# A Strassen–Winograd MLP: unread sums not stored, other sums stored a superblock earlier, an x cast issued earlier, an accumulator in its own tile

## The chip, the cores and the metric

The kernel runs on one core of one Trainium2 chip. The metric is device time in microseconds (us). A smaller time is better.

Names used below: TensorE does the matrix products (PE in the profile), VectorE (DVE) the additions, ScalarE (ACT) copies and gelu, GpSimd (POOL) issues stores to memory, SyncE (SP) issues loads. A "gap" is time in which TensorE sits idle. The granted clock is the share of full speed that TensorE was allowed (1.00 is full). A load or store "lands" when the profile shows its completion.

## The reference

```python
# x: 8 x 1024 x 1024, w1: 1024 x 4096, w2: 4096 x 1024, all float32
def reference(x, w1, w2):
    h = x @ w1
    h = 0.5 * h * (1 + np.tanh(np.sqrt(2 / np.pi) * (h + 0.044715 * h ** 3)))
    return (h @ w2).astype(np.float32)
```

## The kernel before

The 8192 rows of x are taken in eight superblocks of 1024 rows, numbered 0 to 7. In each, two large products (x by w1, then gelu, then by w2) are done with Winograd's form of Strassen's scheme: seven half-size products instead of eight, with sums and differences of blocks as operands. The operand sums of the weights are the same in every superblock, so they are made once on VectorE, stored in device memory and loaded ready-made later.

- w1 is cut in four "quads" of four column chunks. Each quad has four raw blocks (products 2 and 5 use two of them as they are) and five sums, numbered 4, 1, 3, 7, 6.
- w2 has the same five sums. Sums 6 and 7 of w2 are products that are themselves split once more (`split_inner`, stored in `in_d`), so nobody reads the copies of these two sums in `w2_d`.

The first product, cut to what matters. A `MadeQuad` loads raw blocks and makes sums on VectorE; `load_ops` loads the ready operands.

```python
# first product, matmul1
def ahead(q, step):                 # prepares quad q, a part for each chunk of quad q-1
    if q == NI // QC:
        return
    if sb > 2:                      # ready sums from memory
        if step == 0:
            quads.append(load_ops(w1_d[q], raw_d[q], ORDER, KH, QW))
        return
    if step == 0:                   # raw blocks, sums made here; stored in superblock 2
        quad = MadeQuad(q, sb == 0, sb == 2)
        quads.append(quad)
        # ... (superblock 0: load from w1)
    for m in ((), (4,), (1, 3), (7, 6))[step]:
        quads[q].sum(m)             # VectorE, then a store on GpSimd's queue if asked for

for c in range(NI):                 # 16 chunks
    q, j = divmod(c, QC)
    if j == 0:
        ahead(q + 1, 0)
    # ... seven products of the chunk; VectorE combines their results:
    c11 = temp()
    tt(c11, u, rb, ADD)             # the chunk's last combination
    gelu("11", c, c11)
    late = (c, w, qb, s2)
    if j:
        ahead(q + 1, j)             # sums of the next quad
```

The second product of superblocks 0 and 1 (later superblocks use another routine, which loads ready sums):

```python
# matmul2_made
def add(m, over=None):              # one sum of w2, in four pieces
    u, op, v = B_TERMS[m]
    sums[m] = []
    for q in range(NI // QC):
        t = unit(QC, OH) if over is None else raw[over][q]
        tt(t, raw[u][q], raw[v][q], op)
        sums[m].append(t)
        if sb:
            nc.gpsimd.dma_start(out=w2_d[q][:, m - 1, :], in_=flat(t))

# ... products 4 first
u, d = {}, {}
for q, ps in product2(g, 2, pieces(2), pb, False):
    at, d[q] = copy_out("21", q, ps)         # d[q] is one of 10 shared temporaries
    if q == 1:
        xb = x_cast(sb + 1, at)              # casts the next superblock's x, in memory
add(1)
for q, ps in product2(g, 5, pieces(5), qb, True):
    tt(u[q], u[q], ps, SUB)
    tt(d[q], u[q], d[q], SUB)
add(7, over="21")
blocks = x_transpose(xb, load_in_order)
for q, ps in product2(g, 1, pieces(1), rb, True):
    tt(d[q], d[q], ps, ADD)                  # d accumulates output block 22
if sb:
    split_inner(7, pieces(7))
for q, ps in product2(g, 7, pieces(7), rb, False):
    tt(u[q], u[q], ps, ADD)
    store(sb, "11", q, u[q])
# ... products 3 and 6; the last one ends with
    tt(d[q], d[q], ps, ADD)
    last = store(sb, "22", q, d[q])
```

Two buffer pools matter. `tmp` has 10 temporaries of 128 x 512 float32. `u` has 26 buffers for weight operands, blocks of x and staging. A tile scheduler orders the instructions of each engine and inserts the waits for buffers.

## Time and profile before

| | before |
|---|---|
| median of 3 runs | 1582.91 us (1581.23 to 1582.93) |
| span of the profiled execution | 1577.2 us (that execution: 1579.01 us) |
| TensorE busy | 1547.1 us, 98% |
| superblock 0, 1, 2 | 204.53, 195.17, 197.34 us |
| superblocks 3 to 6 | 190.5 us each |

The lengths of superblocks are read from the timeline of TensorE, from the start of one first product to the start of the next. The 190.5 us of a superblock without a gap is the measure for the others.

The first part of the page of before. The columns are busy time, share of the span and number of instructions.

```profile
span 1577.2 us, 20360 instructions
PE 1547.1 (98%) x7808; PEld 767.1 (49%) x7808; DVE 1028.8 (65%) x1291; ACT 467.9 (30%) x784; POOL 202.8 (13%) x290
```

TensorE is the limit. Only the gaps can be won, about 30 us, and some 11 us of these are start-up. The timeline of TensorE for before follows: start, length, engine, line, operation, and in brackets the gap ahead of it and what ended the gap.

```profile
173.87 20.89 PE L567 MATMUL ps<-u,gc 128*128 128x512 f16 x96 [3.02 <-DVE gc L112]
...
222.22 97.37 PE L285 MATMUL ps<-u 128*128 128x512 f16 x448
...
333.79 41.60 PE L567 MATMUL ps<-u,gc 128*128 128x512 f16 x192 [0.38 <-DVE tmp L443]
375.94 13.99 PE L567 MATMUL ps<-u,gc 128*128 128x512 f16 x64 [0.56 <-DVE gc L112]
...
417.39 9.09 PE L285 MATMUL ps<-u 128*128 128x512 f16 x40
431.00 19.20 PE L285 MATMUL ps<-u 128*128 128x512 f16 x80 [4.52 <-ACT tmp L349]
```

The first product of superblock 1 (222.22) runs without a gap worth listing. In superblock 2 TensorE stops for 4.52 us ahead of 431.00. The releaser named is a ScalarE copy, but that is only the last link. VectorE's timeline for before shows the first:

```profile
419.81 2.06 DVE L112 TENSOR_TENSOR tmp<-tmp,ps 128x512 f32<-128x512 f32 x3
427.39 1.22 DVE L112 TENSOR_TENSOR u<-u 128x2048 f16<-128x2048 f16 x1 [5.53 <-DMA u<-raw_d]
428.54 1.28 DVE L112 TENSOR_TENSOR tmp<-tmp,ps 128x512 f32<-128x512 f32 x2
430.98 0.69 DVE L112 TENSOR_TENSOR tmp<-tmp,ps 128x512 f32<-128x512 f32 x1 [1.17 <-ACT tmp L349]
```

`u<-u` at 427.39 is a w1 sum for a later quad. VectorE stood 5.53 us in front of it for a raw block still on its way. The combinations `tmp<-tmp,ps`, which free TensorE's accumulators, stand behind it in the same queue. The table by stage of before (stretch, its length, busy time of each engine with instruction counts; the last three numbers are granted TensorE clock, DMA share and GB/s) shows what surrounded it:

```profile
426.00:430.00 4.00, 0.48 (x3) 0.10 (x1) 2.42 (x3) 0.15 (x1) 1.09 (x3) 1.00 1.02 416
430.00:432.00 2.00, 1.00 (x5) 0.46 (x5) 1.02 (x2) 0.95 (x2) 1.10 (x3) 0.95 1.25 406
432.00:434.00 2.00, 2.00 (x6) 0.69 (x5) 1.41 (x3) 1.24 (x3) 1.03 (x3) 0.50 1.02 330
434.00:436.00 2.00, 2.00 (x8) 0.83 (x7) 0.66 (x2) 0.47 (x1) 0.77 (x2) 0.70 1.04 242
```

DMA was saturated, and after the gap the clock was low. What is missing from full clock in the three stretches from 430 to 436 us (0.05, 0.50 and 0.30 of 2 us each) is 1.7 us, as much as 3.4 us at half clock. One more line of before: the same kind of sum in superblock 1, on VectorE, where the wait was short enough to do no harm.

```profile
227.40 1.23 DVE L112 TENSOR_TENSOR u<-u 128x2048 f16<-128x2048 f16 x1 [1.70 <-DMA u<-raw_d]
```

### The profile page before, as it was taken

To read this page: it belongs to the slowest core of one execution; us is meant where nothing else is said; L and a number is where in the kernel's file an instruction comes from. 1 tells how busy PE (TensorE), PEld (TensorE's weight loads), DVE (VectorE), ACT (ScalarE), POOL (GpSimd) and SP (SyncE) were. 2 spreads that over 40 slices of the span, in tenths; PEclk is the share of its full clock that TensorE was granted. 3 is DMA by queue.
4 is the path that set the end of the run, shared out by engine and by line. 5 is a ranking of instruction groups with operands and counts; after the bars stand their busy time and mean duration, and the time that the engine had idled before them with its cause. 6 is when DMAs were issued, how large, how long until landed. Compare 5 with 4: busy or idle time off the path is not lost.

```text
span 1577.2 us, 20360 instructions
## 1 busy us (share of the span) xinstructions
PE 1547.1 (98%) x7808; PEld 767.1 (49%) x7808; DVE 1028.8 (65%) x1291; ACT 467.9 (30%) x784; POOL 202.8 (13%) x290
## 2 busy tenths in 40 slices
PE   7999999999899999999999999999999999999998
PEld 4444444444344455444554445544554445544454
DVE  6875967678775567555665647656575556655564
ACT  4645024410144111441124410344004430044210
POOL 2241010033310012000120001200121001200000
PEclk9999999999999999999999999999999999999999
DMA  9999852399965567735696446954569445663164
GB/s 303 340 327 340 246 205 97 122 302 327 399 184 144 200 252 271 233 107 191 247 314 200 157 153 246 358 151 179 179 239 355 135 186 192 243 234 134 54 233 167
DMA packets 165634, 352.64 MB, mean 224 GB/s; under 512 B 72736, under 2 KB 78880, under 8 KB 164640
## 3 DMA queue, kind: packets, MB, share of 16 engines
q1 hardware_dynamic: 146944, 278.97, 51.1%
q0 software_dynamic: 18592, 72.37, 13.9%
q8 instruction: 61, 1.00, 0.3%
q14 instruction: 37, 0.30, 0.1%
HBM read 272.63 MB, written 93.32 MB: 232 GB/s over the span
## 4 chain that ended last, share of the span: by engine, by line
PE 86%; DMA 8%; DVE 3%; issue 1%; ACT 1%; POOL 0%; SPq 0%; DVEq 0%; ACTq 0%; POOLq 0%
PE ps L285 47%; PE ps L567 33%; PE ps L523 6%; DMA u<-w_d 2%; DVE u L112 2%; DMA u<-raw_d 2%; DMA gc<-in_w_dram 1%; DVE tmp L112 1%; DMA out_dram<-tmp 1%; DMA in_d<-u 1%; DVE gc L112 1%; DMA w_d<-u 1%; DMA xb<-in_x_dram 0%; DMA u<-in_x_dram 0%; DMA u<-in_d 0%
## 5 line engine op out<-in xcount | busy, mean ns | idle before, releaser
L285 PE MATMUL ps<-u 128*128 128x512 f16 x3584 | 782.1, 380 | 10.5 <-ACT tmp L349 4.5
L112 DVE TENSOR_TENSOR tmp<-tmp,ps 128x512 f32<-128x512 f32 x580 | 395.8, 685 | 301.4 <-ACT tmp L349 113.7
L285 PEld LDWEIGHTS <-u 128*128 128x128 f16 x3584 | 351.5, 98 | 438.6 <-issue 17.2
L567 PE MATMUL ps<-u,gc 128*128 128x512 f16 x1792 | 389.7, 379 | 3.9 <-DVE gc L112 3.6
L567 PEld LDWEIGHTS <-gc 128*128 128x128 f16 x1792 | 175.2, 98 | 216.0 <-DVE gc L112 4.6
L295 ACT ACTIVATE g<-tmp 128x512 f16<-128x512 f32 x256 | 161.0, 630 | 287.4 <-DVE tmp L112 287.4
L567 PE MATMUL ps<-u,g 128*128 128x512 f16 x1024 | 223.6, 379 | 0.0
L112 DVE TENSOR_TENSOR u<-u 128x2048 f16<-128x2048 f16 (+2 forms) x170 | 183.4, 1112 | 20.9 <-DMA u<-raw_d 12.3
L295 ACT ACTIVATE g<-ps 128x512 f16<-128x512 f32 x256 | 151.8, 596 | 98.4 <-PE ps L285 97.8
L567 PEld LDWEIGHTS <-g 128*128 128x128 f16 x1024 | 100.2, 98 | 119.6
L112 DVE TENSOR_TENSOR gc<-g,g 128x2048 f16<-128x2048 f16 x112 | 132.9, 1220 | 15.8 <-PE ps L567 15.8
L112 DVE TENSOR_TENSOR u<-u,ps 128x512 f32<-128x512 f32 x144 | 95.7, 681 | 68.7 <-ACT tmp L624 37.3
L381 POOL DMA_DIRECT2D out_dram<-tmp x72 | 39.5, 548 | 778.4 <-ACT tmp L617 593.1
L523 PE MATMUL ps<-u,gc 128*128 128x256 f16 x960 | 109.8, 273 | 0.7
L349 ACT COPY tmp<-ps 128x512 f32<-128x512 f32 x128 | 73.0, 570 | 95.5 <-PE ps L285 95.5
L523 PEld LDWEIGHTS <-gc 128*128 128x128 f16 x960 | 93.8, 98 | 12.8 <-issue 1.8
L112 DVE TENSOR_TENSOR gc<-u 128x2048 f16<-128x2048 f16 x60 | 73.2, 1219 | 39.3 <-PE ps L567 39.3
L112 DVE TENSOR_TENSOR tmp<-ps,tmp 128x512 f32<-128x512 f32 x128 | 88.2, 689 | 5.9 <-PE ps L285 1.1
L112 DVE TENSOR_TENSOR u<-tmp,ps 128x512 f32<-128x512 f32 x24 | 16.5, 687 | 74.8 <-PE ps L567 65.1
L112 DVE TENSOR_TENSOR u<-g,g 128x2048 f16<-128x2048 f16 x48 | 59.4, 1277 | 0.0
L617 ACT COPY tmp<-ps 128x512 f32<-128x512 f32 x24 | 14.1, 586 | 152.0 <-PE ps L567 152.0
L624 ACT COPY tmp<-ps 128x512 f32<-128x512 f32 x24 | 14.0, 585 | 133.5 <-PE ps L567 132.8
(32 smaller groups left out, 351.0 us busy)
## 6 DMA issues: line engine op xcount, KB each, us to landing
u<-w_d SPq DMA_DIRECT2D x172, 512.0 KB, 7.8
u<-raw_d SPq DMA_DIRECT2D x136, 512.0 KB, 7.1
u<-in_d SPq DMA_DIRECT2D x84, 512.0 KB, 6.8
gc<-in_w_dram SPq DMA_DIRECT2D x48, 512.0 KB, 6.5
w_d<-u POOLq DMA_DIRECT2D x40, 512.0 KB, 7.3
out_dram<-tmp POOLq DMA_DIRECT2D x72, 256.0 KB, 3.8
raw_d<-u SPq DMA_DIRECT2D x32, 512.0 KB, 10.0
xb<-in_x_dram POOLq DMA_DIRECT2D x56, 256.0 KB, 11.0
```

The source lines that it names most:

```text
L112: nc.vector.tensor_tensor(out=out, in0=in0, in1=in1, op=op)
L285: nc.tensor.matmul(bank, lhsT=ops[m][:, k, cs], rhs=xs[m][:, k, :], start=(first and k == 0), stop=(k == KH - 1), skip_group_check=not first,)
L295: gelu_last[0] = nc.scalar.activation(out=g[b][:, c, :], in_=src, func=GELU)
L349: nc.scalar.copy(out=v, in_=pb)
L381: return queue.dma_start(out=out2[r0:r0 + P, o0:o0 + OH], in_=src)
L523: nc.tensor.matmul(bank[:, i * HO:(i + 1) * HO], lhsT=t[:, c, i * P:(i + 1) * P], rhs=y[j][:, c, :], start=(first and i == 0 and c == 0), ...
L567: nc.tensor.matmul(banks[q], lhsT=a, rhs=pieces[c // QC][:, c % QC, :], start=(first and c == 0), stop=(c == NI - 1), skip_group_check=not ...
L617: nc.scalar.copy(out=c21, in_=ps)
L624: nc.scalar.copy(out=c12, in_=ps)
```

## The change

Its intent is to unload superblocks 1 and 2. It has four parts:

1. Sums 6 and 7 of w2 are no longer stored (nobody reads them): eight stores of 512 KB fewer.
2. The sums of w1 quads 1 to 3 are stored in superblock 1, so superblock 2 loads them ready. Only quad 0 stays as it was: 15 VectorE sums fewer.
3. The x cast for superblock 2 stands in the program at the start of superblock 1's second product, in front of its other work, instead of inside it. It need only wait for superblock 0's last output store, and the built program issues it right behind that store: early in superblock 1's first product, against 342.30 us in before.
4. The accumulator `d` of output block 22 gets tiles of its own from the pool `u`, instead of continuing in the shared temporaries.

```diff
-            if sb > 2:
+            if sb > 2 or (sb == 2 and q):
                 if step == 0:
                     quads.append(load_ops(w1_d[q], raw_d[q], ORDER, KH, QW))
                 return
             if step == 0:
-                quad = MadeQuad(q, sb == 0, sb == 2)
+                quad = MadeQuad(q, sb == 0, sb == (1 if q else 2))
@@
-            w = (quads[q] if sb > 2 else quads[q].ops, slice(j * P, (j + 1) * P))
+            w = (getattr(quads[q], "ops", quads[q]), slice(j * P, (j + 1) * P))
@@
-                if sb:
+                if sb and m not in INNER:
                     nc.gpsimd.dma_start(out=w2_d[q][:, m - 1, :], in_=flat(t))
@@
-        u, d = {}, {}
+        u, c21 = {}, {}
+        d = halves()[1]
@@
-            at, d[q] = copy_out("21", q, ps)
-            if q == 1:
+            at, c21[q] = copy_out("21", q, ps)
+            if q == 1 and sb == 0:
                 xb = x_cast(sb + 1, at)
@@
-            tt(d[q], u[q], d[q], SUB)
+            tt(d[q], u[q], c21[q], SUB)
@@
+            xb = x_cast(sb + 1, last) if sb else None
-            last, blocks = matmul2_made(sb, g, None if sb else quad.keep_raw)
+            last, blocks = matmul2_made(sb, g, None if sb else quad.keep_raw, xb)
```

More of the change, by code (lines that the diff above doesn't have):

```diff
@@ L381, in store, with matmul2_made @@
         return queue.dma_start(out=out2[r0:r0 + P, o0:o0 + OH], in_=src)
-    def matmul2_made(sb, g, keep_w1):
+    def matmul2_made(sb, g, keep_w1, xb):
         raw = {b: [] for b in BLOCKS}
```

## The prediction

> **What bounds it now.** TensorE. The page's first part gives PE 1547.1 of 1577.2 us busy (98%), so at most 30 us of gaps can be won. Superblocks 3 to 6 take 190.5 us each without a gap. The gaps (timeline, list of waits): about 11 us of start-up; 3.02 us at 170.9 (superblock 0, second product: VectorE late); 0.38 at 333.4 and 0.56 at 375.4 (superblock 1, second product); 4.52 at 426.5 (superblock 2); 1.92 near the end. Only the middle ones are in reach.
>
> **The gap at 426.5.** VectorE works in order and sat 5.53 us idle until 427.39 for a load of raw w1: an early sum of superblock 2's third quad, queued ahead of chunk work. Behind it waited a chunk's combination, a gelu on ScalarE, then the copy that PE needed. DMA moved 416 GB/s at full share then (table by stage): saturated. After the gap the granted clock was 0.50 in 432 to 434 and 0.70 in 434 to 436; the next 408 matmuls took 90.08 us where the later rate gives 88.2. The stall costs about 4.5 + 1.9 = 6.4 us. The Trainium skill ("TensorE: Matmul & The Clock Gate", Part 1) says a PE idle for about 3.4 us falls to half clock for about as long; the trace agrees (after the 3.02 us gap the clock stayed 1.00).
>
> **What the change does.** Superblock 2 loads quads 1 to 3 ready: 15 sums of 1.23 us (18 us of VectorE) go, three more 512 KB loads per quad come. VectorE no longer waits for raw loads there: the 6.4 us should vanish. The stores of those sums move to superblock 1, whose first product has room (57 to 185 GB/s between 235 and 310). Eight 512 KB stores of w2 sums go, and the x cast leaves the crowded second product of superblock 1: some 0.6 us of gap goes. The accumulator's tile removes a wait of VectorE for an output store (0.41 us at 166), but the built order puts the same work ahead of the late operand, so the 3.02 us gap stays within 0.3 us.
>
> **The cost.** In the built program superblock 0's accumulator tiles are reused at once for sums of quads 1 and 2 of superblock 1, which wait for its last output stores. VectorE reaches them at 221 and 226. The last store issues at about 224 and lands 3.4 us or more later (its median there before), now behind 512 KB stores in its queue; a raw load released by the first of these sums lands 5.9 us after issue, about 228.5. Before, VectorE was free at 227.40, just in time: by the 426 gap, PE resumes 3.6 us after that point, and it runs dry near 230.9. With 228.5 to 230 I estimate a new PE gap of 1 to 3 us near 231, short of the clock penalty.
>
> **Sum.** -6.4 - 0.6 + 2 = -5 us: 1582.9 becomes 1578 us, range 1573.5 to 1583. Faster by over 2%: 0.01; within 2%: 0.98; slower: 0.01.
>
> **Checks.** Right: no PE gap near 426 and clock 1.00 there; 15 fewer VectorE instructions; DMA less saturated in 330 to 390; a PE gap of 1 to 3 us near 231, VectorE waiting for an output store or raw load; 3 us still at 171. Wrong: a gap over 3.4 us near 231 with a clock drop eats the gain; late loads of ready sums stall PE after 441, at superblock 2's fifth chunk; or no new gap: then 1576.

## The result, and the profile after

| | before | after |
|---|---|---|
| median of 4 runs, same rounds | 1582.92 us (1581.23 to 1583.69) | 1579.56 us (1577.43 to 1582.38) |
| ratio after / before | | 0.9981, 95% interval 0.9963 to 1.0000 |
| span of the profiled execution | 1577.2 | 1576.8 |
| superblock 0 | 204.53 | 203.93 |
| superblock 1 | 195.17 | 200.84 |
| superblock 2 | 197.34 | 190.51 |
| superblocks 3 to 6, each | 190.5 | 190.5 |
| superblock 7 | 192.77 | 194.53 |

A ratio is the mean time of one kernel's runs over that of the other's runs of the same rounds, so it is not quite the ratio of the medians in the table. The result is about 0.2% faster.

The superblocks tell more than the total. Superblock 2 gained 6.83 us and superblock 1 lost 5.67 us. The page of after, first part:

```profile
span 1576.8 us, 20365 instructions
PE 1546.9 (98%) x7808; PEld 767.0 (49%) x7808; DVE 1015.0 (64%) x1276; ACT 468.6 (30%) x784; POOL 195.6 (12%) x282
```

VectorE has 15 instructions fewer. The timeline of TensorE for after:

```profile
173.54 20.89 PE L568 MATMUL ps<-u,gc 128*128 128x512 f16 x96 [3.12 <-DVE gc L112]
...
221.90 9.66 PE L285 MATMUL ps<-u 128*128 128x512 f16 x44
235.94 27.12 PE L285 MATMUL ps<-u 128*128 128x512 f16 x116 [4.38 <-DVE tmp L112]
...
339.87 55.41 PE L568 MATMUL ps<-u,gc 128*128 128x512 f16 x256 [0.41 <-DVE tmp L444]
...
422.74 37.50 PE L285 MATMUL ps<-u 128*128 128x512 f16 x173
```

Superblock 2 (422.74) now runs through. A gap of 4.38 us stands in superblock 1, after 44 matmuls, where before had none. VectorE's timeline for after, at that place:

```profile
226.18 0.69 DVE L112 TENSOR_TENSOR tmp<-tmp,ps 128x512 f32<-128x512 f32 x1 [0.80 <-ACT g L295]
233.47 1.23 DVE L112 TENSOR_TENSOR u<-u 128x2048 f16<-128x2048 f16 x1 [6.60 <-DMA out_dram<-u]
234.61 1.28 DVE L112 TENSOR_TENSOR tmp<-tmp,ps 128x512 f32<-128x512 f32 x2
```

It has the same shape as the old gap: a sum for a later quad at the head of VectorE's queue, a long wait, combinations behind it. What it waits for is new. The store of an output tile, `out_dram<-u`, has to land before its buffer may be overwritten. This is the accumulator's own tile (part 4), whose buffer in the pool `u` is handed to the next w1 sums. GpSimd's timeline for after gives the issue of the last of these stores (L381) and the w1 store next to it:

```profile
223.90 0.55 POOL L381 DMA_DIRECT2D out_dram<-u  x1 [1.20 <-DVE u L112]
224.43 0.53 POOL L194 DMA_DIRECT2D w_d<-u  x1
```

Issued at 223.90, landed before 233.47. For the output stores issued between 205 and 240 us, the view of one tensor gives the time to landing. First before, then after:

```profile
DMA to landing us min/median/max: 2.3/3.4/6.6
```

```profile
DMA to landing us min/median/max: 2.3/4.3/9.5
```

The table by stage of after shows the clock after the gap:

```profile
236.00:238.00 2.00, 2.00 (x6) 0.70 (x6) 1.41 (x3) 1.48 (x3) 1.96 (x5) 0.60 0.82 244
238.00:240.00 2.00, 2.00 (x7) 0.75 (x5) 1.05 (x2) 0.27 (x2) 0.00 (x0) 0.55 1.30 317
```

The first product of superblock 1 became 6.37 us longer (97.21 us from its start to the start of the second product before, 103.58 after): 4.38 us of this gap, 0.17 us of a second small one, and about 1.8 us left over, which is the lowered clock (the two stretches above lack 1.7 us of full clock). The second product became 0.70 us shorter. Together this is the 5.67 us.

The two profiled executions differ by 0.4 us only, the medians by 3.4. The profiled execution of before, at 1579.01 us, was 3.9 us below the median of its timed runs, so its profile shows one of its good executions.

### The profile page after: what moved, and what is told of

The parts are those of the page before. It is cut to its first block, busy times and chain, and to the rows that moved or that the text cites. A ratio compares the mean times of both kernels' runs of the same rounds, so it can differ in the third digit from the quotient of the medians.

```text
span 1576.8 us, 20365 instructions
## 1 busy us (share of the span) xinstructions
PE 1546.9 (98%) x7808; PEld 767.0 (49%) x7808; DVE 1015.0 (64%) x1276; ACT 468.6 (30%) x784; POOL 195.6 (12%) x282
## 4 chain that ended last, share of the span: by engine, by line
PE 79%; DMA 3%; DVE 3%; issue 1%; ACT 0%; SPq 0%; DVEq 0%
PE ps L285 41%; PE ps L568 31%; PE ps L524 6%; DMA u<-w_d 2%; DVE u L112 1%; DMA u<-raw_d 1%; DVE gc L112 1%; DVE tmp L112 1%; DMA u<-in_d 0%; DVE tmp L444 0%; ACT tmp L618 0%; SPq L381 0%; DVEq L112 0%; SPq L513 0%
## 5 line engine op out<-in xcount | busy, mean ns | idle before, releaser
L112 DVE TENSOR_TENSOR tmp<-tmp,ps 128x512 f32<-128x512 f32 x564 | 385.6, 686 | 307.6 <-ACT tmp L349 117.2
L112 DVE TENSOR_TENSOR u<-u 128x2048 f16<-128x2048 f16 (+2 forms) x155 | 166.5, 1110 | 11.9 <-DMA out_dram<-u 6.6
L112 DVE TENSOR_TENSOR u<-u,ps 128x512 f32<-128x512 f32 x160 | 106.5, 681 | 85.4 <-ACT tmp L625 37.3
L381 POOL DMA_DIRECT2D out_dram<-tmp x64 | 35.1, 549 | 811.9 <-ACT tmp L618 636.2
```

The lines of the kernel that those rows point to most:

```text
L112: nc.vector.tensor_tensor(out=out, in0=in0, in1=in1, op=op)
L381: return queue.dma_start(out=out2[r0:r0 + P, o0:o0 + OH], in_=src)
```

## The experiments

Twelve runs were made, eleven of edited kernels and one of after unedited, all correct, all profiled and timed in five rounds. e1, e2, e3 and e5 share one set of runs of before (median 1582.43 us), the kernel after run again, e4, e6 and e7 another (1582.86), e8 and e9 a third (1580.84), e10 and e11 a fourth (1582.28). They are told by question, not by number. "Gap near 231" and "gap near 426" mean the two places above, whatever the exact time in that run.

### Is the result itself repeatable?

The kernel after, unedited, run again.

> The changed kernel once more, unedited, for a tighter ratio on the same chip as the next three. Expected ratio 0.998, a gap of 3.5 to 4.5 us near 231 with a clock drop, none near 426. Whether the clock also drops after the 3.1 us gap near 171 may differ from run to run (it did in two of the first four experiments and not in the others), which would spread the times by some 1.7 us.

Measured: 1579.51 us, ratio 0.9977 (0.9953 to 1.0000). The gap near 231 was 4.07 us, superblock 2 took 190.51. The result repeats, though both intervals reach 1.0000. This profile fell on a slower execution (span 1580.7), and it shows one reason for the spread. TensorE's timeline of this run:

```profile
174.90 22.58 PE L568 MATMUL ps<-u,gc 128*128 128x512 f16 x96 [3.12 <-DVE gc L112]
```

The same 3.12 us gap, the same 96 matmuls: 20.89 us in the first profile of after, 22.58 here. The table by stage has the clock at 0.50 in 176 to 178 us and 0.67 in the next 2 us, where the profile of before had 1.00 throughout. After a gap of this length the clock drops in some executions and not in others.

### Which part makes the gap near 231?

Two parts were suspect: the w1 stores in superblock 1 (more traffic in the store queue) and the accumulator's tile (a buffer that an output store holds). The x cast also moved. One experiment takes the tile out of after, one puts the tile alone into before, one takes the x cast's move out, one takes the w1 stores' move out.

```diff
# e1_acc_in_temps: after, accumulator in the shared temporaries again
-        u, c21 = {}, {}
-        d = halves()[1]
+        u, d = {}, {}
-            at, c21[q] = copy_out("21", q, ps)
+            at, d[q] = copy_out("21", q, ps)
-            tt(d[q], u[q], c21[q], SUB)
+            tt(d[q], u[q], d[q], SUB)
# e2_acc_tile_only: before, with only this part, the same lines the other way round
# e3_xcast_back: after, x cast issued as before
-            if q == 1 and sb == 0:
+            if q == 1:
-            xb = x_cast(sb + 1, last) if sb else None
+            xb = None
# e5_w1_back: after, sums of w1 stored in superblock 2 again
-            if sb > 2 or (sb == 2 and q):
+            if sb > 2:
-                quad = MadeQuad(q, sb == 0, sb == (1 if q else 2))
+                quad = MadeQuad(q, sb == 0, sb == 2)
```

> The changed kernel, but with the accumulator of superblocks 0 and 1 back in the temporaries of the output copies. Theory A (reuse): in the changed kernel a sum of superblock 1's third quad takes the accumulator's place and so waits for the last output store; without the tile that wait is gone. Expected: no PE gap over 1 us near 231, none near 426, ratio to the kernel before about 0.996 (some 6 us won). Theory B (traffic): the stores of sums and the x cast, moved early, crowd the DMA queues and the third quad's raw loads come late whatever the accumulator does. Expected: a PE gap of 3 to 5 us near 231 stays, now with a raw load as releaser, ratio 0.998 to 1.000.

> The kernel before with only the accumulator's own tile added. Theory A (reuse alone): the gap near 231 appears in full (about 4 us and a clock drop) beside the old one near 426: ratio about 1.003. Theory B (traffic): nothing new near 231, ratio 1.000. Both needed (reuse makes the sum wait for the store, traffic makes the store land late): the store lands about 3.5 us after its issue, so the gap near 231 is 0 to 1.5 us, ratio 1.000 to 1.001. The gap near 426 stays in all cases.

> The changed kernel, but with the x cast of superblock 1 issued in its second product as before; the early stores of sums and the accumulator's tile stay. If the x cast's traffic is what makes the last output store land 9.5 us after issue, the store lands in 4 to 6 us and the gap near 231 falls to under 2 us; if the stores of sums do it, the gap stays at 3 us or more. DMA near 330 to 390 is full again, with up to 1 us of PE gaps there. Ratio 0.996 to 0.998.

> The changed kernel, but with the sums of w1 stored in superblock 2 as before; the early x cast and the accumulator's tile stay. Near 231: if the stores of sums ahead of it in its queue hold up the last output store, it now lands within 5 us of issue and the gap is under 1.5 us; if the x cast does, the gap stays at 3 us or more. Near 426 VectorE again waits for raw loads; the x cast is out of the way there, so that gap may be as long as before (4.5 us and a clock drop) or shorter. Ratio 0.999 to 1.004.

Measured:

| kernel | median us | ratio (95%) | gap near 231 | gaps near 426 |
|---|---|---|---|---|
| after, run again | 1579.51 | 0.9977 (0.9953 to 1.0000) | 4.07 | none |
| e1, after without the tile | 1577.03 | 0.9974 (0.9960 to 0.9989) | 2.44 | none |
| e2, before with the tile | 1590.88 | 1.0064 (1.0049 to 1.0079) | 2.87 | 3.30 and 3.16 |
| e3, after, x cast as before | 1581.07 | 0.9995 (0.9981 to 1.0009) | 4.43 | none |
| e5, after, w1 stored late | 1586.95 | 1.0036 (1.0020 to 1.0051) | 2.06 | 3.08 and 3.07 |

Without the tile, VectorE's wait near 231 is for a raw load, as in before, but longer:

```profile
231.12 1.23 DVE L112 TENSOR_TENSOR u<-u 128x2048 f16<-128x2048 f16 x1 [4.16 <-DMA u<-raw_d]
```

Not all of this was expected. The gap of e1, 2.44 us, lay between its two theories, and so did that of e5; e2 cost twice what its worst theory said; e3 gained less than expected. What follows:

- The gap near 231 has two sources. With neither early w1 stores nor a tile (before) there is none; with the early stores, the early x cast and no tile 2.44 us (e1); with the tile alone 2.87 us (e2); with both 4.07 to 4.43 us. They overlap rather than add, because VectorE waits for the later of two things at the same place.
- With the tile in place the x cast has no part in it: 4.43 us with it moved back (e3), against 4.38, and the last output store took 9.5 us to land in both. Whether it has a part in the 2.44 us of e1 was not tested. Its early issue may be worth something (0.9995 against 0.9977), but the intervals overlap.
- The slow store does not need the moved traffic. In e2 nothing was moved, and the last output store still took 8.2 us to land; in e5, without the early w1 stores, 7.4 us. So these stores in its queue are not the only cause; without them the landing was about 2 us shorter. The raw loads of the next quad, four of 512 KB issued at 222.8 to 224.5 us, run in the same stretch (mean DMA share 0.91 in 224 to 230 us of e2); that these delay the store is likely, but no run took them away.
- The tile alone makes the kernel 0.64% slower. It also makes superblock 2 worse, since the same accumulator of superblock 1 holds buffers there: VectorE waits 4.74 and 6.80 us for its output stores. TensorE's timeline of e2, superblock 2:

```profile
430.45 7.62 PE L285 MATMUL ps<-u 128*128 128x512 f16 x28 [3.30 <-DVE tmp L112]
441.23 9.03 PE L285 MATMUL ps<-u 128*128 128x512 f16 x28 [3.16 <-DVE tmp L112]
```

- The gain of superblock 2 comes from part 2. Taking it back (e5) brings two gaps and loses 0.6%. But these are not the gap of before come back: VectorE's sums wait there 4.52 and 6.60 us for the tile's output stores, as in e2, and not for raw loads as expected. So e5 shows what part 2 is worth with the tile in place.

### Is it bandwidth, or the order on VectorE?

At both places a sum for a later quad stands in front of a combination that is needed at once. If order is the cause, it must be enough to hold each sum behind the chunk's last combination, with all traffic kept. If bandwidth is the cause, TensorE must still run dry.

```diff
# e4_after_pinned: after; e6_before_pinned: before; the same edit
-        nc.vector.tensor_tensor(out=out, in0=in0, in1=in1, op=op)
+        return nc.vector.tensor_tensor(out=out, in0=in0, in1=in1, op=op)
+        chunk_last = [None]
-                quads[q].sum(m)
+                if chunk_last[0] is None or sb == 0:
+                    quads[q].sum(m)
+                    continue
+                with tc.issue_after(chunk_last[0].ins):
+                    quads[q].sum(m)
-            tt(c11, u, rb, ADD)
+            chunk_last[0] = tt(c11, u, rb, ADD)
```

> The changed kernel with one thing more: from superblock 1 on, VectorE may issue a sum of w1 for the next quad only behind the combination that ends the present chunk, so no sum stands ahead of chunk work while its data is still on the way. Theory (the head of VectorE's queue): slot reuse and traffic only hurt because a waiting sum blocks in-order work behind it. Expected: no PE gap near 231 nor near 426, clock 1.00 there; against the changed kernel 4.4 + 1.6 us less: ratio to before 0.994 to 0.995. Rival (the data itself is late): PE stalls later instead, near 245 when quad 1 or near 270 when quad 2 starts, and the ratio stays at 0.998.

> The kernel before with the same ordering rule alone, none of the change. If the 4.5 us gap near 426 was the order of VectorE's queue and not a lack of DMA bandwidth, it goes although all the traffic stays: ratio 0.995 to 0.996. If the bandwidth was the limit, the gap stays or moves to the start of quads 1 and 2 of superblock 2 (near 441 and 466): ratio 0.998 to 1.000.

Measured: e4 1576.39 us, ratio 0.9956 (0.9931 to 0.9981); e6 1578.02 us, ratio 0.9972 (0.9935 to 1.0009, one of its six runs at 1592.64), so the time of e6 alone is not clear of before's. Both gained a little less than expected. Both gaps are gone in both kernels. For e6, first a line of TensorE's timeline (superblock 2's first product), then two stretches of the table by stage:

```profile
418.67 31.68 PE L285 MATMUL ps<-u 128*128 128x512 f16 x146
```

```profile
408.00:418.00 10.00, 10.00 (x48) 4.50 (x46) 5.38 (x6) 0.00 (x0) 3.29 (x7) 1.00 1.02 411
418.00:426.00 8.00, 8.00 (x38) 3.63 (x37) 3.54 (x6) 2.88 (x5) 3.98 (x8) 1.00 1.08 381
```

DMA is as full as in before (381 to 411 GB/s, share over 1), and TensorE does not stop. The gap near 426 needed the order of VectorE's queue; full DMA alone does not make it. The raw loads were late here too (one that was issued at 418.00 landed at 428.3), but nothing that TensorE needed then depended on them. The rule does shift some traffic: the last of these four raw loads was issued at 436.99, against 419.92 in before.

The rule does not take away everything. The gap ahead of 96 matmuls near 171 us stays (3.12 in e4, 2.90 in e6), and in both runs the clock dropped after it (22.58 us). And e4 has a gap of 2.29 us near 335, e6 one of 1.85, where before and after had about 0.4; the held-back work probably arrives together elsewhere, but this was not tested.

### A version without either

The gap near 171 has a like cause in the second product: the four pieces of `add(7)` stand in VectorE's queue ahead of the difference that product 1 needs as its next left operand. They are needed only by product 7. VectorE's timeline of before, the four pieces and then the differences:

```profile
166.86 4.62 DVE L112 TENSOR_TENSOR u<-u 128x2048 f16<-128x2048 f16 x4
...
172.59 3.49 DVE L112 TENSOR_TENSOR gc<-g,g 128x2048 f16<-128x2048 f16 x3
```

```diff
# e7_pinned_late_add: e4, and
-        add(7, over="21")
         blocks = x_transpose(xb, load_in_order)
         for q, ps in product2(g, 1, pieces(1), rb, True):
             tt(d[q], d[q], ps, ADD)
+        with tc.issue_after(gc_last[0].ins):
+            add(7, over="21")
# product2, where the left operand's difference is made
-                tt(a, g[u][:, :, cols], g[v][:, :, cols], SUB)
+                gc_last[0] = tt(a, g[u][:, :, cols], g[v][:, :, cols], SUB)
```

> The changed kernel with that ordering rule, and in superblocks 0 and 1 the four w2 sums of product 7 also held behind the last left operand of product 1. The 3.1 us gap near 171 should go, and with it the clock drop that follows it in some runs: ratio 0.991 to 0.993 (another 3.1 us, and up to 1.7 us in some runs), with a narrower spread of the times. This should be the fastest of all.

Measured: 1567.73 us (1566.95 to 1569.83), ratio 0.9901 (0.9874 to 0.9929). It is faster than both kernels, by a little more than expected, and its runs lie within 2.9 us. There is no gap over 0.3 us between 160 and 450 us. TensorE's timeline of this run:

```profile
159.66 31.03 PE L575 MATMUL ps<-u,gc 128*128 128x512 f16 x143
...
218.15 96.86 PE L286 MATMUL ps<-u 128*128 128x512 f16 x448
...
328.66 55.48 PE L575 MATMUL ps<-u,gc 128*128 128x512 f16 x256
...
411.60 38.58 PE L286 MATMUL ps<-u 128*128 128x512 f16 x178
```

Is the tile what makes this possible, or is it idle weight here too? The same kernel, accumulator back in the temporaries, with the lines of e1:

> The fastest version (ordering rule and late last addition), with the accumulator back in the shared temporaries. My account: the accumulator's own tile gives nothing once the order is held, so the time is within 1.5 us of 1567.7 and the ratio 0.989 to 0.991; no tensor engine gap over 0.5 us between 160 and 450 us. Rival (the tile is what keeps the corrected order free of waits): a gap on the tensor engine waiting for the temporaries or the vector engine comes back in superblock 1, and the time rises by over 2 us to a ratio above 0.9915.

Measured: 1570.72 us (1569.33 to 1573.24), ratio 0.9932 (0.9911 to 0.9952). The interval overlaps that of e7. The profile is 1.9 us longer (span 1567.9 against 1566.0); gaps of 1.11 and 0.35 us came back in superblock 2 near 424, VectorE waiting 4.4 us in two for output stores from the temporaries, and one of 0.48 in superblock 1. The time lies on the rival's side of the line that was drawn, but the gaps it expected in superblock 1 did not come. So the tile, harmful under the original order, probably gives 2 us under the corrected one; the timing does not settle it.

And is the change itself still worth anything once the order is held? Before, with the rule and the late addition and nothing of the change:

```diff
# e11_before_pinned_late: before, with the edits of e6 and of e7
```

> The kernel before with only the ordering rule and the late last addition of the fastest version, nothing of the change. Theory A (with the order held, the whole change is worth only the small gaps of superblock 1's second product and the x cast): the 3 us gap near 171 is gone, a gap of 1 to 2.5 us stays in superblock 1 near 334, none near 231 or 426, and the ratio is 0.991 to 0.994, so 1 to 4 us above 1567.7. Rival B (the early stores and loads of the change matter to the fastest version): over 5 us above 1567.7, ratio above 0.9945, with a gap of over 2 us in superblock 1 or 2 at which the tensor engine waits for the vector engine.

Measured: 1577.86 us (1572.95 to 1585.24), ratio 0.9972 (0.9940 to 1.0004), profiled span 1574.0. The rival was right. The gap near 171 is gone, but superblock 2 takes 197.09 us. TensorE's timeline of e11, then VectorE's:

```profile
420.30 8.75 PE L286 MATMUL ps<-u 128*128 128x512 f16 x32 [2.82 <-DVE tmp L112]
430.82 19.37 PE L286 MATMUL ps<-u 128*128 128x512 f16 x89 [1.77 <-DVE tmp L112]
```

```profile
430.08 1.48 DVE L112 TENSOR_TENSOR tmp<-tmp,ps 128x512 f32<-128x512 f32 x2 [2.78 <-DMA out_dram<-tmp]
```

With the order held, it is a combination itself that waits, for a temporary which an output store has not yet left. GpSimd's timeline of that stretch has w1 stores, output stores and the next superblock's x cast interleaved. The five w1 stores among them are quad 0's, which the change leaves where they are: e7 has the same five there, and its output stores land as slowly (6.0 to 11.9 us, against 6.1 to 12.0 in e11). But in e7 they leave from the accumulator's tile, so no combination waits for them; in e9, without the tile, combinations wait again. For these gaps the traces thus point to the tile, though e6, also without it and without the late addition, had none. e7 is 0.7% better by the ratios than e11; how that divides among the four parts was not tested further. Neither the change alone (0.998), nor the order alone (0.997), comes near the two together (0.990).

### Do the unread stores matter?

My account by now gave all to parts 2 and 4 and to order. It held the unread w2 stores (part 1) for harmless. Two experiments: after with these stores back, and before without them.

```diff
# e8_w2_back: after, with
-                if sb and m not in INNER:
+                if sb:
# e10_w2_only: before, with the same line the other way round
```

> The kernel after, but the sums 6 and 7 of w2, which nothing reads, are stored again. My account (these stores cost neither the tensor engine nor the vector engine anything that matters; only the queue carries more): within 0.5 us of the kernel after, so a ratio of 0.997 to 0.9995 to the kernel before; superblock 2 stays at 190.5 us; the gap near 231 stays at about 4.4 us. Rival (the bandwidth that the unread stores took was part of the cost): a gap of over 1 us comes back in superblock 1 or 2 beyond those of the kernel after, and the time is 1 us or more above it.

> The kernel before with one part of the change alone: the unread sums 6 and 7 of w2 are not stored. The run with these stores put back into the kernel after lost 12.5 us in one gap, because a vector engine operation of the superblock's second product waited for the store that frees its buffer. Theory A (the unread stores do harm only together with the w1 stores that the change moves ahead of them): superblock 1 loses its two small gaps (0.38 and 0.56 us) and little else, the gap near 426 stays at over 3 us, and the ratio is 0.997 to 1.000. Rival B (the unread stores are most of the whole change's gain by themselves): the gap near 426 shrinks below 1 us too, and the ratio is 0.994 to 0.9965.

Measured: e8 1593.04 us (1590.98 to 1596.22), ratio 1.0075 (1.0052 to 1.0097). I had expected 0.997 to 0.9995. Even the rival, with a loss of 1 us or more, had not foreseen the size: 13.5 us above after, by the medians of different rounds. Superblock 1 took 214.73 us, against 200.84 in after. TensorE's timeline, VectorE's, and a stretch of the table by stage, all of e8:

```profile
397.38 12.21 PE L568 MATMUL ps<-u,gc 128*128 128x512 f16 x48 [12.46 <-DVE gc L112]
```

```profile
377.12 1.22 DVE L112 TENSOR_TENSOR gc<-g,g 128x2048 f16<-128x2048 f16 x1
390.30 0.69 DVE L112 TENSOR_TENSOR u<-u 128x1024 f16<-128x1024 f16 x1 [11.96 <-DMA in_d<-u]
```

```profile
385.00:397.00 12.00, 0.00 (x0) 0.00 (x0) 4.00 (x6) 0.00 (x0) 1.05 (x2) 0.59 1.34 212
```

VectorE stood 11.96 us in front of a sum of the inner split, for a buffer whose store to `in_d` had not landed; TensorE's left operand stood behind it. The stores to `in_d` of the stretch 360 to 400 us landed after a median of 15.2 us in e8 and of 3.5 us in after.

Taking the same stores out of before (e10) gave 1582.32 us, ratio 0.9995 (0.9964 to 1.0025), inside what theory A expected. Its profile lost the 0.56 us gap near 375, had 0.65 us in place of the 0.38, and kept one of 4.12 near 426, with VectorE waiting 5.82 us for a raw load. It also had 4.72 us near 171, in code that this edit does not reach.

So the unread stores cost next to nothing in before, and 13 us in the presence of the other three parts. With which of these they collide was not tested: no run has them with one part alone, save e2 (the tile), which has only 1.24 us ahead of the same 48 matmuls. The moved w1 stores are not in the traffic of that stretch: in e8 the last of them landed at 286.8 us, before the first sum of w2 was stored (300.22). What did move into it are the transposed loads of the next x, which the early cast (part 3) lets start some 27 us sooner (with the cast moved back, in e3, they start at 363.1). SyncE's timeline of before, after and e8:

```profile
356.24 30.61 SPq L120 DMA_TRANSPOSE u<-xb  x16
```

```profile
329.12 25.87 SPq L120 DMA_TRANSPOSE u<-xb  x16
```

```profile
328.91 67.00 SPq L120 DMA_TRANSPOSE u<-xb  x16
```

Together with the unread stores these 16 loads took a median of 19.4 us each to land in e8, against 4.5 in after, and were spread over 67 us. So part 3 is the likelier partner; the run that would show it, e8 with the x cast as before, was not made. Either way, a part that is worth nothing by itself is not idle in the whole.

## Why the prediction was right or wrong

The total was right: 1578.0 predicted, 1579.56 measured, inside the range. Step by step:

- **The gap at 426 costs 6.4 us and vanishes: right.** Superblock 2 went from 197.34 to 190.51 us, 6.83 less, and the clock stayed at 1.00. The cause named (an early sum in VectorE's queue) was shown by e6. "DMA saturated" was true but not enough by itself: e6 removed the gap with the same stores and loads kept.
- **0.6 us of small gaps go in superblock 1: right in substance.** The 0.56 gap went; the 0.38 became 0.41; the second product of superblock 1 became 0.70 us shorter. The 0.56 goes with part 1: e10 alone lost the 0.56. The x cast's share was not separated.
- **The gap near 171 stays within 0.3 us: right** (3.02 to 3.12).
- **15 VectorE instructions fewer: right** (1291 to 1276). **DMA less saturated in 330 to 390: right for two of three stretches.** The DMA share was 0.90, 1.07, 1.08 in steps of 20 us before, and 1.07, 0.43, 0.59 after.
- **A new gap of 1 to 3 us near 231, without a clock drop: the mechanism right, the size wrong.** TensorE ran dry at 231.56 (predicted 230.9). VectorE waited for the output store of the accumulator's tile, as foreseen. But the gap was 4.38 us and the clock fell to 0.55 to 0.60 after it. The mis-sized term is the landing of the last store: issued at about 224, it "lands 3.4 us or more later". 3.4 us was the median of the output stores there; this one took 9.5 us. The very same store of before had already taken 6.6 us, the maximum in the same line of the profile, most likely because it meets the next quad's raw loads (the five stores before it took 2.3 to 5.2 us). I took a median of six stores for the one store that mattered. One term erred the other way: TensorE resumed 2.47 us after VectorE's sum began at 233.47, where 3.6 us was predicted; otherwise the gap would have been longer still. By its own checks the prediction had named this outcome as the wrong one (a gap over 3.4 us near 231 with a clock drop). Superblock 1 became 5.67 us longer instead of about 2.
- **The sum of -5 us: in range partly by luck.** It was therefore about -1.2 us in superblocks 1 and 2 of the profiled pair (+5.67 - 6.83). The medians fell by 3.4 us, nearer to the prediction than the term that failed would suggest. The profile of before was one of its good executions, and the clock after some gaps of both kernels drops in some executions only (below). How the remaining 2 us divide between these is not settled: only the one profile of each set of runs is there. The stated range, 1573.5 to 1583 us, also holds a change of nothing, so the total does not confirm the terms.
- **What I left out:** the removal of the unread stores was costed at the gaps it frees. That it protects superblock 1 from a 12 us gap, once the rest of the change is in, was found only by e8. Also left out: the early cast lets the transposed loads of x start in the middle of superblock 1's second product.

On the clock, the prediction leaned on the Trainium skill ("TensorE: Matmul & The Clock Gate", Part 1): a window of about 3.4 us, free-running, after which an idle TensorE falls to half clock. The runs agree with the halved clock (0.50) and show that a gap need not be 3.4 us. A free-running window would fit the differences between executions told next, but no run shows the window itself. Of ten profiles with a gap of 2.90 to 3.12 us near 171, five show the drop after it (22.58 us for the next 96 matmuls) and five do not (20.89). Near 231, 2.44 and 2.87 us (e1, e2) were followed by a clock of 0.72 in 234 to 240, and 2.06 us (e5) was not. At the start of superblock 7's first inner product even 2.02 us was. TensorE's timeline of after and a stretch of its table by stage:

```profile
1515.61 2.88 PE L524 MATMUL ps<-u 128*128 128x256 f16 x16 [2.02 <-DMA u<-in_d]
```

```profile
1517.00:1519.00 2.00, 2.00 (x11) 1.40 (x10) 0.00 (x0) 0.42 (x1) 0.00 (x0) 0.50 0.99 318
```

In before the 16 matmuls at this place took 1.92 us, after a gap of 1.92. The extra length of superblock 7 in after (1.76 us) begins here, in code that the change does not touch. In these runs the drop after a gap of 2 to 3 us was thus a matter of luck, worth up to 1.7 us each time.

## What to carry to other kernels

When work for later stands in an in-order engine's queue ahead of work that is needed now, hold it back by an ordering rule before buying bandwidth: here the rule took away the two stalls that it aimed at, with all loads and stores kept (smaller ones came up elsewhere), and with the change and the late addition it gave 1%. When a tile is moved to a pool with long-lived stores in front of its next use, cost the landing of the particular store which frees the buffer, in the traffic that it meets, not the median of its kind. Parts of a change must also be tested inside the whole: removing the unread stores was worth nothing alone and 13 us in company.

## What the Trainium skill lacked or had wrong

- "TensorE: Matmul & The Clock Gate", the table of its section "Why this matters for your kernels", advises no idle gaps over about 3 us. Here gaps of 2.02, 2.44 and 2.87 us were each followed by a clock near or at half, and gaps of 2.90 to 3.12 us in five of ten profiles. The page has the free-running window, but not that a single gap of 2 to 3 us drops the clock in some executions. One drop cost 1.7 us (22.58 against 20.89 us for 96 matmuls).
- "DMA: Bandwidth & Descriptors", "Anatomy of one DMA — SWDGE (gpsimd) path", fits the time of one transfer as about 2.0 us plus bytes over 436 GB/s. For a store of 256 KB that is an estimate of 2.6 us. The fastest output store of the window took 2.3 us, which is near it; the median was 3.4 to 4.3, and the one that counted took 6.6 to 9.5 us. In e8 stores of 256 and 512 KB had a median of 15.2 us. The page doesn't say that its fit is for a quiet queue, and gives no landing time for a store in a shared, full one.
- No page consulted says that holding work for later behind urgent work on VectorE can remove a stall during which DMA is saturated (e6: 381 to 411 GB/s, no gap).
